# A transformer block on one core: a seventh blocked tile in the MLP's up stage, its weight sums requested before the tile ahead, and the down stage's block sums built later

## The chip, the cores and the metric

The kernel runs on one core of one Trainium2 chip. The metric is the device time of one execution in microseconds (us), as the median of several runs. All arithmetic is in 32-bit floats. The engines of the core are TensorE (PE, the matmuls; PEld is its weight load), VectorE (DVE), ScalarE (ACT), GpSimd (POOL) and SyncE (SP), which here only issues transfers. POOL also issues transfers: those that add to what already lies at the destination.

## The reference

One decoder block over 512 tokens of width 1024: a norm, a mixed attention, a gated MLP with a short causal convolution, and a gate with a second input. The part that matters here is the MLP:

```python
h = rmsnorm(x, mlp_pre_g[i])
gu = h @ w_gate_up[i].astype(h.dtype)          # 1024 -> 2 * 2816
a, u = jnp.split(gu, [D_FF], axis=-1)
a = causal_dwconv(a, conv_w[i], conv_b[i])     # 3 taps along the tokens
y = (jax.nn.gelu(a, approximate=True) * u) @ w_down[i].astype(h.dtype)   # 2816 -> 1024
x = x + rmsnorm(y, mlp_post_g[i])
```

## The kernel before

Data lies transposed: 128 features on the partitions, 512 tokens along the free axis. Each float matrix is kept as two parts, a rounded high part and a remainder, and every product is three matmuls (high by high, low by high, high by low). A weight therefore goes through four steps: a load into a raw place ("wr", two places), the high part by an ACT copy (line 144), the low part by a DVE subtraction (line 148), and then the matmuls (lines 165, 168, 169). The split parts lie in six "wh" places, two for each weight of 1024 columns.

**The up stage** (`mlp_up`) walks over 22 tiles j of 128 features of `w_gate_up`, from about 250 us of the profiled execution on. A *plain* tile has two weights, gate and up, each multiplied in 8 steps of the inner dimension, so 2 x 8 x 3 = 48 matmuls of 512 columns. A *blocked* tile (list `BLOCKED`, line 73) computes the same outputs by the seven-product scheme for a 2 x 2 block of matrices (`blocked_tile`, line 1249): 7 products of 4 steps, 84 matmuls of 256 columns. It needs sums of quarter weights and sums of quarter inputs, and more additions at the end to put the four output blocks together (lines 1268 to 1274). After each tile of either kind come the convolution (ACT line 1155, DVE line 1157 twice), the gelu (ACT line 1158), the product with the other half (line 1177, or 1276 in a blocked tile), and the split of the result y (lines 1163 and 1164).

**The weight sums** of a blocked tile are made by transfers alone (`block_sums_ahead`, line 1205). Two tiles x and y of 512 KB are taken from the places with tag "p" (six). SP loads quarter weights into them (lines 1211 and 1212). Then POOL issues three adding transfers, one after another (`accumulate`, line 1203): y += two quarters from memory, a half of x += a half of y, the other half of x += the first. The three additions are placed behind the last matmul issued so far (`self.pinned`), but that is an order for the planner and no wait on the chip. In `blocked_weights` (line 1235) a blocked tile uses four weights in this order: two raw quarters from memory (line 1239), y, one raw quarter (lines 1241 to 1245), x.

**The down stage** (`mlp_down`) multiplies y by `w_down`. Six of its eight output tiles go in pairs by the same blocked scheme. For one of the pairs the weight sums are prepared in memory (`downblocks`): four copies of 384 KB from memory to memory, issued by SP (`down_copies`, line 1227, through line 291), then four adding transfers from POOL (`down_additions`, line 1233, through line 1203). The third adds what the second has made, and the fourth what the third has made. `group_weights` reads them at line 1076. The kernel before calls two copies after blocked tile 10 and two after blocked tile 12. The additions are called in threes from the end of tile `DOWN_SUMS` on.

**The order.** A planner lays the program out ahead of time. It simulates the engines, takes the ready instruction that stands first in the program, and gives each tile a free place of its tag, or a wait until one is freed. On the chip each engine then works its instructions strictly in that order. An instruction whose input is not there holds up all that stand behind it on its engine. `load_late` (line 291) keeps a transfer behind all that the program has given to SP before it.

**Places.** `SLOTS` gives how many places each tag has. `YTAG` says where the 22 results y lie until the end of the down stage, `PTAG` where the sums of the inputs lie, `TTAG` where the sums of y lie in the down stage. `mlp_down` names tags for the last weights of the down stage and for the first weights of the gate (lines 1381 to 1386).

Of the kernel before, what the change touches and what calls it, by code (L numbers as in the profile page):

```python
# [42 lines left out]
SLOTS = {"u": 26, "kn": 4, "p": 6, "pt": 3, "tt": 2, "wh": 6}  # L43


YTAG = ["u"] * 18 + ["kn"] * 3 + ["p"]


NB = 4
# [16 lines left out]
MP = 3  # L66
ORDER = [[(0,), (), (1, 2)], [(0,), (1, 2), ()], [(0, 1, 2), (), ()]]
STAG = ["u", "u", "u", "tt", "tt", "tt"]
TTAG = ["pt"] * 3 + ["p"] * 5 + ["u"] * 4
LAGS = [(1, 2), (2, 2)]  # L70


BLOCKED = [10, 12, 14, 16, 18, 20]
ROWS = 2048
RAW_LAST = 6
PTAG = ["pt", "pt", "pt", "tt", "tt", "p", "p", "kn"]
AHEAD = 8
DOWN_SUMS = 16
DRAM_SUMS = 1


class Block:
# [977 lines left out]
    def sums_of(self, i):  # L1060
        f = self.u([P, 2, T], F32, STAG[i])
        for k in range(2):
            y = self.y[2 * i + k]
            self.nc.vector.tensor_add(f[:, k, :], y[:, 0, :].bitcast(F32), y[:, 1, :].bitcast(F32))
        self.tt.append([self.u([P, 2, T], F32R, t) for t in TTAG[2 * i : 2 * i + 2]])
        for _ in self.half_sums([[f[:, k, hs] for hs in HALF] for k in range(2)], self.u([P, 4, H], F32, STAG[i]), self.tt[i]):
# [93 lines left out]
    def keep_y(self, j, c):  # L1160
        nc = self.nc
        y = self.u([P, 2, T], F32R, YTAG[j])
        nc.scalar.activation(y[:, 0, :], c, AF.Copy)
# [41 lines left out]
    def block_sums_ahead(self, j):  # L1205

        gs = self.io["gs"][BLOCKED.index(j)]
        two = lambda t: t.rearrange("p (s n) -> p s n", s=2)
# [26 lines left out]
    def blocked_weights(self, j):  # L1235

        nc, gs = self.nc, self.io["gs"][BLOCKED.index(j)]
        x, y = self.ahead_sums.pop(j)
# [58 lines left out]
    def mlp_up(self):  # L1297
        self.phase = "mlpup"
        nc, io = self.nc, self.io
        self.y = []  # L1300
        self.tt = []
        self.hn, self.ht = [], []
        x1 = self.x1
        pss = self.chunkwise(self.upw, self.h2, ("s", "mm", "s", "mm"))
        raws = []
        for i in range(2):
            raws.append(self.u([P, D], F32, "p"))
            self.load_late(raws[i], io["gu"][NB + 2 + i])
        ahead = [self.weight(io["gu"][NB + i], keep=True) for i in range(2)]
        ahead += [self.weight(r, early=True) for r in raws]  # L1310
        self.spill()
        cyc = itertools.cycle(["s", "o", "t", "t", "s", "mm", "s", "mm"])
        pp = {}
        n = 0
        self.ahead_sums = {}
        todo = self.normalized(x1)
        copies, adds = self.down_copies(), None
        for j in range(NB // 2, NFF):
            if j == AHEAD:
                self.block_sums_ahead(BLOCKED[0])  # L1320
            if j in BLOCKED:
                for _ in todo:
                    pass
                self.blocked_tile(j, [next(cyc) for _ in range(4)])
                if j != BLOCKED[-1]:
                    self.block_sums_ahead(BLOCKED[BLOCKED.index(j) + 1])
                for _ in range(2):
                    next(copies, lambda: None)()
            else:
                x = self.h2 if j <= RAW_LAST else self.hn  # L1330
                for i in range(2):
                    wt = ahead.pop(0) if ahead else self.weight(io["gu"][2 * j + i])
                    ps = self.ps(next(cyc))
                    self.ordered = n < 4
                    self.gemm(ps, wt, x)
                    self.ordered = False
                    pp[i] = ps
                    if n == 0:
                        self.r3 = self.row_rstd(self.row_sums(self.acc3), "r3")
                        for k in range(NB // 2):  # L1340
                            self.mlp_tile(k, pss[2 * k], pss[2 * k + 1])
                    n += 1
                    if n > 1:
                        for _ in range(1 if j <= RAW_LAST else 2):
                            next(todo, None)
                self.mlp_tile(j, pp[0], pp[1])
            if j >= DOWN_SUMS:
                for c in copies:
                    c()
                adds = adds or self.down_additions()  # L1350
                self.pinned = self.last
                for _ in range(3):
                    next(adds, lambda: None)()
                self.pinned = None
        for a in adds:
            a()

    def mlp_down(self):
        self.phase = "mlpdown"
        nc, io = self.nc, self.io  # L1360
        acc = self.s([P, T])
        yo = [self.u([P, 2, T]) for _ in range(4)]
        ks = [range(0, 8), range(8, 16), range(16, NFF)]
        self.pgw = []
        self.rawtag = itertools.cycle(["wr", "wr", "kn"])
        for c in range(2 * MP, KC - 1):
            m = yo[c // 2][:, c % 2, :]
            ps = self.ps("mm")
            for n, k in enumerate(ks):
                wt = self.weight(io["down"][c][:, k.start * P : k.stop * P], len(k) * P)  # L1370
                self.gemm(ps, wt, [self.y[j] for j in k], k.start == 0, k.stop == NFF)
                self.sums_of(n)
            nc.vector.tensor_copy(m, ps)
            self.square_acc(acc, m, True)
        for c in range(0, 2 * MP, 2):
            self.pair_of_tiles(c, yo[c // 2], acc)

        c = KC - 1
        keep = self.tc.keep_in_program_order
        wts = []  # L1380
        for k, t in zip(ks, ("wr", "wr", "u")):
            n = len(k) * P
            wts.append(self.weight(self.raw(io["down"][c][:, k.start * P : k.stop * P], n, t), n, early=True))
        for n, tag in enumerate((("p", "tt"), ("pt", "pt"), ("kn", "tt"))):
            self.pgw.append(self.weight(io["wpg"][n], tag=tag))
        raw = self.raw(io["wpg"][3])
        self.e = self.unspill("e", ["pt", "u", "u", "u"])

        def last(h, js, ps):
            for j in js:  # L1390
                self.mm3(ps, wts[j // 8], j % 8 * P, self.y[j][:, :, HALF[h]], j == 0, j == NFF - 1, keep=True)

        def out(h, ps):
            m = yo[c // 2][:, c % 2, HALF[h]]
            sq = self.s([P, H])
            keep(nc.scalar.activation(sq, ps, AF.Square))
            keep(nc.vector.tensor_copy(m, ps))
            a = acc[:, HALF[h]]
            keep(nc.vector.tensor_add(a, a, sq))
            return a  # L1400

        ps0, ps1 = (self.ps(t)[:, HALF[h]] for h, t in enumerate(("s", "mm")))
        last(0, range(NFF), ps0)
        a0 = out(0, ps0)
        last(1, range(5), ps1)
        y = self.rstd_col(a0, "r4a")
        last(1, range(5, 10), ps1)
        r = self.rstd_row(y, "r4a", copy=False)
        self.pgw.append(self.weight(raw, early=True, keep=True))
        last(1, range(10, NFF), ps1)  # L1410
        self.phase = "norm"
        self.x2 = []
        run = lambda gen, n: [next(gen, None) for _ in range(n)]
        first = self.norm_half(0, r, C_GMPOST, yo, self.x1, self.x2)
        run(first, 4)
        a1 = out(1, ps1)
        self.pss = [self.ps(t) for t in ("s", "s", "s", "mm")]
        run(first, 1)
        self.gate_half(0, range(0, 3))
        y = self.rstd_col(a1, "r4b")  # L1420
        run(first, 2)
        self.gate_half(0, range(3, 5))
        r = self.rstd_row(y, "r4b", copy=False, tag="o")
        run(first, 2)
        second = self.norm_half(1, r, C_GMPOST, yo, self.x1, self.x2)
        run(second, KC + 1)
        self.gate_half(0, range(5, KC))
        self.gate_half(1, range(KC))
# [36 lines left out]
    def run(self):  # L1465
        self.consts()
        self.attention()
        self.tc.cur_priority = LATE
        self.out_proj()
        self.mlp_up()  # L1470
        self.mlp_down()
        self.ple_gate()
# [62 lines left out]
```

## Time and profile before

| what | value |
|---|---|
| runs shown | 660.81, 660.32 and 664.28 us, median 660.81 |
| profiled execution | 660.37 us, its span 658.7 us |
| busy DVE, ACT, POOL | 74%, 54%, 26% of the span |
| DMA over the span | 93.37 MB, mean 142 GB/s |
| up stage, tiles 10 to 21 | 360.0 to 490.6 us of the span |
| down stage and the rest | from 490.6 us on |

A profile line of an engine names the line of the code, the engine and the operation, then what is written and read by the program's names with numbers left out, and the shape: `mlpup_wh<-mlpup_wr` is a split weight made from a raw one, `mlpup_u` any tile of the pools "u", "p", "kn", "pt" or "tt", `in_gs_dram` the quarter weights of blocked tiles, `in_gu_dram` those of plain tiles. `[2.79 <-DMA ...]` is idle time in front of an instruction, and what ended it. SPq and POOLq are the issuing queues of SP and POOL. A row of the chain of waits has a start, a length, and what took it. A row of transfers has a count, the size of one and the median us from issue to landing.

### The profile page before, as it was taken

The numbers are of one execution on the slowest core, as the hardware profiler recorded it, in microseconds if no ns is written. First come the engines' busy times: TensorE is split into PE (matmuls) and PEld (weight loads), VectorE is DVE, ScalarE is ACT, GpSimd is POOL, SyncE is SP. The second block draws the span as 40 slices with busy tenths as digits, with TensorE's granted clock in tenths as the row PEclk, the third lists the DMA queues.
The fourth block names the chain that finished last, engine by engine and source line by source line (L and its number), as shares of the span: only waits on it lengthen the run. The fifth ranks groups of instructions, "written<-read, shape, count | busy, mean of one in ns | idle before, by whom it ended". The sixth has DMA issues, their size and how long they took to land.

```text
span 658.7 us, 10426 instructions
## 1 busy us (share of the span) xinstructions
PE 647.8 (98%) x3665; PEld 562.9 (85%) x3665; DVE 485.2 (74%) x995; ACT 357.8 (54%) x664; POOL 171.5 (26%) x253
## 2 busy tenths in 40 slices
PE   9999999999999999999999999989999999999997
PEld 8988878878888888888888988879988899999986
DVE  6795687978756469689998576477699775856873
ACT  7464687978887476345556245345544443334351
POOL 1111597678486060002221112101000010201000
PEclk9999999999999999999999999999999999999999
DMA  8436721212264437321259976985252434387032
GB/s 303 158 115 202 199 66 46 58 27 62 69 210 157 146 102 281 129 96 65 96 144 275 234 178 180 215 228 144 65 144 80 145 89 121 91 279 275 3 112 81
DMA packets 41252, 93.37 MB, mean 142 GB/s; under 512 B 4336, under 2 KB 13680, under 8 KB 40944
## 3 DMA queue, kind: packets, MB, share of 16 engines
q1 hardware_dynamic: 37440, 84.75, 39.7%
q0 software_dynamic: 3616, 7.87, 7.0%
q8 instruction: 29, 0.48, 0.3%
q14 instruction: 23, 0.19, 0.1%
q10 hardware_dynamic: 144, 0.08, 0.1%
HBM read 75.91 MB, written 9.44 MB: 130 GB/s over the span
## 4 chain that ended last, share of the span: by engine, by line
PE 87%; DVE 5%; ACT 3%; DMA 3%; issue 2%; POOL 1%; DVEq 0%; ACTq 0%
PE mlpup_pss L168 3%; PE mlpup_pss L169 3%; PE mlpup_pss L165 3%; DMA mlpup_wr<-in_gs_dram 3%; PE mlpup_pst L165 2%; PE mlpup_pst L168 2%; PE mlpup_pst L169 2%; PE nsa_pso L609 2%; PE nsa_pst L576 2%; PE mlpdown_psmm L165 2%; PE mlpdown_psmm L168 2%; PE mlpdown_psmm L169 2%; PE mlpup_psmm L165 2%; PE mlpup_psmm L168 2%; PE mlpup_psmm L169 2%; PE mlpdown_pst L169 2%
## 5 line engine op out<-in xcount | busy, mean ns | idle before, releaser
L144 ACT ACTIVATE mlpup_wh<-mlpup_wr 128x1024 fp32r<-128x1024 f32 x32 | 33.7, 1055 | 51.4 <-DMA mlpup_wr<-in_gs_dram 30.3
L148 DVE TENSOR_TENSOR mlpup_wh<-mlpup_wr,mlpup_wh 128x1024 fp32r<-128x1024 f32 x32 | 39.9, 1246 | 27.0 <-ACT mlpup_wh L144 23.9
L144 ACT ACTIVATE mlpdown_wh<-mlpdown_wr 128x1024 fp32r<-128x1024 f32 (+1 forms) x27 | 26.7, 989 | 46.9 <-PE mlpdown_psmm L168 11.0
L148 DVE TENSOR_TENSOR mlpdown_wh<-mlpdown_wr,mlpdown_wh 128x1024 fp32r<-128x1024 f32 (+1 forms) x27 | 31.5, 1165 | 20.7 <-ACT mlpdown_wh L144 20.7
L287 POOL TENSOR_TENSOR mlpdown_s<-mlpdown_s,mlpdown_s 128x512 f32<-128x512 f32 x6 | 9.7, 1617 | 137.3 <-ACT mlpdown_s L286 137.1
L599 POOL TENSOR_SCALAR nsa_u<-nsa_u,nsa_nrc,gate 128x512 f32<-128x512 f32 (+3 forms) x64 | 38.6, 615 | 14.7 <-DVE nsa_nrc L735 9.6
L701 ACT ACTIVATE nsa_u<-nsa_u,nsa_nnm 128x512 f32<-128x512 f32 (+3 forms) x64 | 35.4, 555 | 6.8 <-DVE nsa_nnm L694 6.6
L168 PE MATMUL mlpup_pss<-mlpup_u,mlpup_wh 128*128 128x256 f32 (+1 forms) x100 | 33.8, 338 | 2.8 <-DVE mlpup_wh L148 2.8
L581 DVE TENSOR_TENSOR nsa_u<-nsa_pst,nsa_u 128x512 fp32r<-128x512 f32 (+1 forms) x43 | 29.4, 685 | 6.8 <-ACT nsa_u L578 6.5
L165 PE MATMUL mlpup_pss<-mlpup_u,mlpup_wh 128*128 128x256 f32 (+1 forms) x100 | 33.5, 335 | 0.0
L169 PE MATMUL mlpup_pss<-mlpup_u,mlpup_wh 128*128 128x256 f32 (+1 forms) x100 | 33.3, 333 | 0.0
L1158 ACT ACTIVATE mlpup_s<-mlpup_s 128x512 f32<-128x512 f32 x22 | 13.9, 631 | 32.6 <-DVE mlpup_s L1157 32.4
L148 POOL TENSOR_TENSOR fill_wh<-fill_wr,fill_wh 128x1024 fp32r<-128x1024 f32 (+2 forms) x13 | 24.5, 1887 | 26.5 <-ACT fill_wh L144 26.5
L1174 POOL TENSOR_TENSOR mlpup_s<-mlpup_s,r3b 128x512 f32<-128x512 f32 x7 | 11.1, 1580 | 78.0 <-ACT mlpup_s L1158 78.0
L168 PE MATMUL mlpup_pst<-mlpup_u,mlpup_wh 128*128 128x512 f32 (+1 forms) x92 | 31.1, 338 | 0.0
L165 PE MATMUL mlpup_pst<-mlpup_u,mlpup_wh 128*128 128x512 f32 (+1 forms) x92 | 31.1, 338 | 0.0
L169 PE MATMUL mlpup_pst<-mlpup_u,mlpup_wh 128*128 128x512 f32 (+1 forms) x92 | 30.9, 338 | 0.0
L694 DVE CUSTOM_DVE_ANT_0 nsa_u<-nsa_pss,biastables_u 128x224 f32<-128x224 f32 (+3 forms) x64 | 27.8, 447 | 3.0 <-PE nsa_pss L635 2.4
L578 ACT ACTIVATE nsa_u<-nsa_pst 128x512 fp32r<-128x512 f32 x43 | 25.4, 593 | 8.5 <-PE nsa_pst L576 8.1
L168 PE MATMUL mlpup_psmm<-mlpup_u,mlpup_wh 128*128 128x512 f32 (+1 forms) x80 | 26.9, 337 | 0.4 <-DVE mlpup_wh L1245 0.4
L165 PE MATMUL mlpup_psmm<-mlpup_u,mlpup_wh 128*128 128x512 f32 (+1 forms) x80 | 26.9, 337 | 0.2 <-ACT mlpup_wh L1244 0.2
L1203 POOL DMA_DIRECT2D mlpup_u<-mlpup_u x12 | 10.6, 886 | 62.6 <-DMA mlpup_u<-in_gs_dram 30.8
(548 smaller groups left out, 2350.9 us busy)
## 6 DMA issues: line engine op xcount, KB each, us to landing
mlpup_wr<-in_gu_dram SPq DMA_DIRECT2D x26, 512.0 KB, 3.3
mlpup_u<-in_gs_dram SPq DMA_DIRECT2D x12, 512.0 KB, 4.6
mlpdown_wr<-in_down_dram SPq DMA_DIRECT2D x7, 512.0 KB, 3.6
fill_wr<-in_win_dram SPq DMA_DIRECT2D x6, 512.0 KB, 3.7
mlpup_u<-in_gs_dram POOLq DMA_DIRECT2D x6, 512.0 KB, 7.1
mlpup_u<-mlpup_u POOLq DMA_DIRECT2D x12, 256.0 KB, 3.7
mlpup_wr<-in_gs_dram SPq DMA_DIRECT2D x6, 512.0 KB, 6.1
fill_u<-fill_u SPq DMA_DIRECT2D x20, 128.0 KB, 2.7
```

Source lines behind the costliest of these rows:

```text
L144: h = nc.scalar.activation(hi, raw, AF.Copy)
L148: l = eng.tensor_sub(lw, raw, hi.bitcast(F32))
L165: r = self.pin(mm(ps, hi, x[:, 0, :], start=start, stop=False))
L168: mm(ps, lo, x[:, 0, :], start=False, stop=False)
L169: self.last = mm(ps, hi, x[:, 1, :], start=False, stop=stop).ins
L576: self.att(nc.tensor.transpose(pt[:, r * P : (r + 1) * P], src, self.ident))
L578: nc.scalar.activation(t[:, 0, :], pt, AF.Copy)
L581: nc.vector.tensor_sub(t[rs, part, :], pt[rs], t[rs, 0, :].bitcast(F32))
L599: self.nc.gpsimd.tensor_scalar(ap, ap, col, gate, op0=ALU.mult, op1=ALU.mult)
L694: nc.vector.tensor_tensor_reduce(dst, src, dist, op0=ALU.add, op1=ALU.min, scale=SLOPES[8 + 4 * g + r], scalar=start, accum_out=out)
L701: nc.scalar.activation(dst, dst, AF.Exp, bias=nm[:, r, b : b + 1], scale=-1.0, accum_out=sm[:, r, b : b + 1])
L1158: nc.scalar.activation(c, c, AF.Gelu_apprx_tanh)
```

## The change

- `BLOCKED` has seven tiles instead of six: 10, 12, 13, 15, 16, 18, 20. Tile 14 becomes plain, and 13 and 15 become blocked, so 12 and 13 are neighbours, and 15 and 16.
- In `mlp_up` the sums of the next blocked tile are asked for before `blocked_tile` and not after it. When they are asked for, the tile ahead still holds its own x and y.
- The two calls of copies after a blocked tile go. `DOWN_SUMS` goes from 16 to 18, and there all four copies are called at once, at the end of tile 18, with three additions behind them, and the fourth at tile 19.
- Tags: y of tile 17 lies in "kn" instead of "u", and y of tile 20 in "p" instead of "kn". One sum tile of the down stage goes from "p" to "u". The third raw weight of the last down tile goes from "u" to "tt", and the first gate weight from "p" and "tt" to "u" and "u".
- The host lays out `in_gs_dram` for seven tiles (line 1507, which reads the list).

```diff
-YTAG = ["u"] * 18 + ["kn"] * 3 + ["p"]
+YTAG = ["u"] * 17 + ["kn"] * 3 + ["p"] * 2
...
-TTAG = ["pt"] * 3 + ["p"] * 5 + ["u"] * 4
+TTAG = ["pt"] * 3 + ["p"] * 4 + ["u"] * 5
...
-BLOCKED = [10, 12, 14, 16, 18, 20]
+BLOCKED = [10, 12, 13, 15, 16, 18, 20]
...
-DOWN_SUMS = 16
+DOWN_SUMS = 18
...
-                self.blocked_tile(j, [next(cyc) for _ in range(4)])
                 if j != BLOCKED[-1]:
                     self.block_sums_ahead(BLOCKED[BLOCKED.index(j) + 1])
-                for _ in range(2):
-                    next(copies, lambda: None)()
+                self.blocked_tile(j, [next(cyc) for _ in range(4)])
...
-        for k, t in zip(ks, ("wr", "wr", "u")):
+        for k, t in zip(ks, ("wr", "wr", "tt")):
...
-        for n, tag in enumerate((("p", "tt"), ("pt", "pt"), ("kn", "tt"))):
+        for n, tag in enumerate((("u", "u"), ("pt", "pt"), ("kn", "tt"))):
```

## The prediction

> **What bounds the kernel now.** I read the page's busy times first, then a table of busy time cut at the starts of the up stage's tiles, then the chain of waits, then the transfers.
>
> ```profile
> PE 647.8 (98%) x3665; PEld 562.9 (85%) x3665; DVE 485.2 (74%) x995; ACT 357.8 (54%) x664; POOL 171.5 (26%) x253
> ```
>
> TensorE (PE) is busy for 647.8 of 658.7 us. Only two things can shorten the kernel: fewer matmul columns, or less of PE's lost time. The next rows are tiles 12 to 19 of the up stage, one row each. The columns are the stretch, its length, then busy time and instruction count of PE, PEld, DVE, ACT and POOL, the granted clock, the DMA share and GB/s.
>
> ```profile
> 380.92:392.06 11.14, 10.29 (x86) 10.08 (x85) 8.41 (x11) 6.57 (x10) 1.22 (x1) 1.00 0.61 151
> 392.06:402.96 10.90, 10.90 (x50) 9.02 (x49) 6.19 (x11) 3.49 (x5) 1.77 (x2) 1.00 0.84 220
> 402.96:413.47 10.51, 10.28 (x86) 10.07 (x84) 8.21 (x10) 5.94 (x9) 2.92 (x3) 1.00 0.69 150
> 413.47:424.38 10.91, 10.91 (x51) 9.02 (x50) 4.10 (x8) 1.77 (x2) 1.75 (x2) 1.00 0.96 241
> 424.38:437.84 13.46, 11.15 (x85) 10.30 (x84) 9.20 (x12) 7.07 (x11) 2.70 (x3) 1.00 0.90 224
> 437.84:448.75 10.91, 10.91 (x51) 9.02 (x49) 8.56 (x12) 5.13 (x7) 1.17 (x2) 1.00 0.80 197
> 448.75:458.74 9.99, 9.99 (x85) 9.99 (x84) 7.67 (x12) 4.91 (x7) 0.86 (x1) 1.00 0.48 130
> 458.74:469.65 10.91, 10.91 (x51) 9.02 (x49) 7.99 (x11) 5.31 (x8) 0.00 (x0) 1.00 0.26 75
> ```
>
> A plain tile (48 matmuls of 512 columns) takes 10.91 us. A blocked one (84 of 256) takes 9.99 us when nothing waits, as tile 18 does. Tiles 12, 14 and 16 take 11.14, 10.51 and 13.46: they lose 1.15, 0.52 and 3.47 us, together 5.14. The clock is 1.00 throughout, so these are waits. The chain says for what:
>
> ```profile
> 390.32 6.94 DMA mlpup_wr<-in_gs_dram
> ...
> 411.73 9.93 DMA mlpup_wr<-in_gs_dram
> ...
> 433.73 1.23 DVE mlpup_wh L148
> 435.00 0.39 PE mlpup_pss L168
> ```
>
> A 9.93 us load of a blocked tile's raw weights stands ahead of the late split on DVE (L148) for which PE waits at 435.00. ACT is the link. In the list of waits from 340 to 440 us it stands idle for such loads:
>
> ```profile
> ACT mlpup_wh L144 <- DMA mlpup_wr<-in_gs_dram: 24.3, 3, 9.2
> ```
>
> While ACT waits, the convolution and gelu of the tiles before stand queued behind the split, and then everything comes at once. The loads themselves are slow because of what is in flight beside them. The transfers issued from 364 to 369 us, and then from 399 to 414 us, with the median us to landing last:
>
> ```profile
> downblocks<-in_gd_dram SPq DMA_DIRECT2D x2, 384.0 KB, 6.5
> ...
> mlpup_wr<-in_gs_dram SPq DMA_DIRECT2D x1, 512.0 KB, 8.4
> ```
>
> ```profile
> downblocks<-in_gd_dram POOLq DMA_DIRECT2D x2, 384.0 KB, 8.9
> ...
> mlpup_wr<-in_gs_dram SPq DMA_DIRECT2D x1, 512.0 KB, 9.9
> ```
>
> In the first group the down stage's copies run beside the load of tile 12, in the second its additions beside the load of tile 16.
>
> **The change, part by part.**
>
> *One more blocked tile.* The list goes from six to seven. PE gains 10.91 - 9.99 = 0.92 us.
>
> *Weight sums ahead.* The call moves in front of the tile. What it can change shows in the timeline:
>
> ```profile
> 357.57 1.23 DVE L148 TENSOR_TENSOR mlpup_wh<-mlpup_u,mlpup_wh 128x1024 fp32r<-128x1024 f32 x1 [0.26 <-ACT mlpup_wh L144]
> ...
> 358.83 0.38 SPq L1211 DMA_DIRECT2D mlpup_u<-in_gs_dram  x1
> ...
> 379.72 0.87 POOL L1203 DMA_DIRECT2D mlpup_u<-mlpup_u  x1 [2.79 <-DMA mlpup_u<-mlpup_u]
> ...
> 401.77 1.04 ACT L144 ACTIVATE mlpup_wh<-mlpup_u 128x1024 fp32r<-128x1024 f32 x1
> ```
>
> ```profile
> mlpup_u<-mlpup_u POOLq DMA_DIRECT2D x12, 256.0 KB, 3.7
> ```
>
> The load at 358.83 starts 0.03 us after the split of tile 10's sum has ended (357.57 + 1.23), and it is for tile 14. Tile 12's places are already taken. So the trace already runs two blocked tiles ahead, in four of the six "p" places, and the moved call finds the same place free at the same moment. I take nothing for it, gain or loss. Its cover: tile 14's last addition is issued at 379.72 and lands 3.7 us later, at 383.4, 24.6 us after the first load; the sums are first split at 401.77, 18 us after that. In the new list that place goes to tile 13, due one plain tile (10.91) and tile 12's saved wait (1.15) earlier, so 6 us are left. Tiles 15, 16 and 18 likewise come 2 x 9.99 + 10.91 = 30.9 us after the tile whose places they take, against the 24.6 needed. If that cover went, PE would lose each sum's lateness in full. On POOL, additions of two tiles stand in order behind each other; on SP the two loads stand ahead of the tile's own raw loads, as they do now.
>
> *Copies and additions to tile 18.* These rows give first and last starts:
>
> ```profile
> L291 SPq DMA_DIRECT2D downblocks<-in_gd_dram x4: 508/578/1418, 346.9 to 366.8; - x4
> L1076 SPq DMA_DIRECT2D mlpdown_u<-downblocks x3: 367/409/462, 488.9 to 518.6; - x3
> ...
> L1203 POOL DMA_DIRECT2D downblocks<-downblocks x2: 807/984/1161, 421.5 to 427.5; - x2
> ```
>
> Four copies on SP and four additions on POOL leave the stretch 347 to 428 us. The copies now follow tile 18's raw loads on SP. The chain has the raw load of tile 16 at 411.73, 12.7 us before that tile; tile 18 starts at 448.75 - 5.14 - 0.92 = 442.7 in the new time, so the copies go out from about 430 us, at the latest with the tile. Two additions follow, then one, then one: 430 + 6.5 + 3 x 8.9 = 463 us for the last landing, at the latest 476. The first reader, at 488.9 now, comes at 483 at best. I cost them at nothing: 7 to 20 us cover them, and beyond that every us late would be PE's. What they free is most of the 5.14 us, but tiles 18 and 20, which lose nothing now, get the traffic.
>
> *Neighbouring blocked tiles, 12 with 13 and 15 with 16.* This is the new load. A blocked tile moves 512 + 256 KB of raw weights, three times 512 KB for its sums, and twice 256 KB between places: 2.9 MB. A plain one moves 1.05 MB. Tiles 12 to 16 are four and one, 12.6 MB in 4 x 9.99 + 10.91 = 50.9 us: 248 GB/s. In the table, 241 GB/s had a DMA share of 0.96 and the slowest load. So the removal of the down traffic is partly refilled. I bound the new loss s: 0 as in tile 18, or 3.47 in each of 13, 15, 16 and 18 as in tile 16, so 13.9 us. Nearest are tiles 12 and 14, whose loads took 8.4 and 6.94 us without the pile-up of tile 16; their mean loss is (1.15 + 0.52)/2 = 0.84. I take that for 13, 15 and 16, and 0 for 12 (its copies are gone), 18 and 20: s = 2.5.
>
> Where a page disagrees: the Trainium skill, "DMA: Bandwidth & Descriptors", Specifications, gives some 358 GB/s of memory bandwidth for a core. By that, 248 would be two thirds of what is there, no load would queue, and s would be 0. The row with 0.96 at 241 GB/s speaks against it here, so I do not take it as the forecast.
>
> *Places by other tags.* One y from "u" to "p", one sum tile from "p" to "u", one raw weight to "tt", one gate weight to "u": the same work in as many places. The cover is the same idle ACT and DVE in the down stage; I take nothing.
>
> **The sum.** The profiled execution took 660.37 us, its span 658.7; the median of the three runs is 660.81, 0.44 above. Relative to the median: 660.81 - 0.92 - 5.14 + 2.5 = 657.25, so 657.2.
>
> **The rivals.**
>
> 1. *The transfers stay quick, full gain.* s = 0: 660.81 - 6.06 = 654.8. For it: the down traffic goes, and tile 13's raw loads are issued into a quiet stretch (0.61 in the row of tile 12). Against: 248 GB/s. This is the skill's case above.
>
> 2. *DVE takes the place of the load.* The rows by shape for 392 to 413 us:
>
> ```profile
> L148 DVE TENSOR_TENSOR mlpup_wh<-mlpup_wr,mlpup_wh 128x1024 fp32r<-128x1024 f32 x4 | 4.9, 1223 | 5.5 <-ACT mlpup_wh L144 5.5
> ...
> L1274 DVE TENSOR_TENSOR mlpup_s<-mlpup_pso,mlpup_s 128x512 f32<-128x512 f32 x1 | 0.7, 682 | 0.0
> ...
> L1269 DVE TENSOR_TENSOR mlpup_s<-mlpup_s,mlpup_pss 128x256 f32<-128x256 f32 x1 | 0.4, 414 | 0.0
> ```
>
> A blocked tile has one wide split, three instructions of 512 and three of 256 columns more than a plain one: 1.22 + 3 x 0.68 + 3 x 0.41 = 4.5 us. Tiles 12 to 19 in the table have 60.3 us of DVE for four pairs, 15.1 each, so a plain tile has 5.3 and a blocked one 9.8, beside PE's 9.99. If DVE also stands idle for 2.3 us a tile, as in tile 18's row (9.99 - 7.67), the second tile of each pair is 2.1 us late: 4.2 us, with 0.84 each for 15 and 18 s = 5.9, and the time 660.7. Against: the gaps can be filled by splits, and plain tile 14 lets DVE catch up.
>
> 3. *Slower: the raw loads queue behind the sums through the whole stretch.* ACT waits at 13, 15, 16 and 18 as it did at 16, 3.47 us each: 654.75 + 13.9 = 668.6. It decides from s = 6.06 us on. For it: 248 GB/s, and only two raw places, refilled about 10 us ahead. Against: the down traffic that made tile 16 so slow is gone, and a load that waits longer needs over 10 us to hurt.
>
> **How the numbers follow.** Forecast with partial gain 0.55; full gain 0.15; DVE 0.20; slower 0.10. The range 654.8 to 662.0 starts at s = 0 and ends at 3.47 in both 15 and 16 (654.75 + 6.94, 661.7, rounded up); about 2 in 10 lie outside. Within 1%, about what a measurement here can tell from no change, means 654.2 to 667.4. Faster by more needs idle time that no term here holds: 0.04. Slower by more is half of rival 3: 0.05. Same: 0.91.
>
> **What would show it.** The changed table should have seven blocked rows. Right: 12 near 9.99, and 13, 15 and 16 below 11.2; DMA share above 0.85 from 12 to 16; ACT's total wait for raw blocked loads below 24.3 us. Wrong: any blocked row above 13, PE waiting on a downblocks load in the down stage, a POOL addition that ends after its split is due, or the row of 18 as slow as that of 16 was. An up stage under 125 us from tile 10's start on would be the full gain.

## The result, and the profile after

| | median us | runs from to | profiled execution | its span |
|---|---|---|---|---|
| before | 661.11 | 660.32 to 664.28 | 660.37 | 658.7 |
| after | 654.33 | 654.24 to 654.43 | 654.41 | 652.7 |

The ratio is 0.9889, with a 95% interval of 0.9856 to 0.9921. The changed kernel is faster by 1.1%. The forecast of 657.2 was wrong, and 654.33 lies 0.5 us below its range. The first rival, the full gain at 654.8, came closest.

The first row of the page after gives the busy times of the engines:

```profile
PE 645.0 (99%) x3701; PEld 563.1 (86%) x3701; DVE 489.3 (75%) x1002; ACT 359.7 (55%) x667; POOL 174.4 (27%) x256
```

Next are tiles 12 to 19 of the up stage after, one row each, with the columns of the table in the prediction. The sum below them is that of all twelve tiles, 10 to 21.

```profile
380.38:390.84 10.46, 10.26 (x85) 10.05 (x84) 8.97 (x12) 5.80 (x9) 1.22 (x1) 1.00 0.70 143
390.84:400.84 10.00, 10.00 (x86) 10.00 (x85) 8.33 (x12) 5.94 (x8) 2.04 (x3) 1.00 1.00 336
400.84:411.75 10.91, 10.91 (x50) 9.02 (x49) 8.12 (x13) 4.53 (x6) 1.87 (x2) 1.00 0.83 171
411.75:421.74 9.99, 9.99 (x85) 9.99 (x84) 7.55 (x12) 4.90 (x7) 2.09 (x2) 1.00 0.90 205
421.74:431.74 10.00, 10.00 (x86) 10.00 (x85) 6.25 (x9) 5.44 (x8) 1.59 (x3) 1.00 0.93 288
431.74:442.65 10.91, 10.91 (x50) 9.02 (x49) 10.08 (x15) 5.06 (x8) 1.41 (x2) 1.00 0.97 276
442.65:452.64 9.99, 9.99 (x85) 9.99 (x84) 8.27 (x13) 5.06 (x7) 3.47 (x4) 1.00 0.80 164
452.64:463.55 10.91, 10.91 (x50) 9.02 (x49) 5.52 (x7) 4.39 (x6) 1.57 (x2) 1.00 0.89 218
...
sum 124.97, PE 124.77 PEld 115.10 DVE 93.95 ACT 59.22 POOL 19.14; mean PE 10.40 PEld 9.59 DVE 7.83 ACT 4.93 POOL 1.60
```

Only tile 12 still loses anything, 10.46 - 9.99 = 0.47 us. Before, the same twelve tiles took from 360.02 to 490.55, so 130.53 us; now they take 124.97. These 5.56 us are the whole effect of the change: what comes after the up stage takes 168.1 us before (658.7 - 490.6) and 168.2 us after. The other 0.5 us between the two spans stands ahead of tile 10, which begins at 359.48 and not at 360.02. No part of the change lies there, and that start moves by as much from one kernel to the next in all the experiments below.

The heavy traffic that the prediction feared did come: over tiles 12 to 16 the DMA engines move 227 GB/s at a share of 0.87. Tile 13 runs at a DMA share of 1.00 and 336 GB/s, tiles 16 and 17 at 0.93 and 0.97. ACT still stands idle for raw weights of blocked tiles (its waits from 340 to 440 us):

```profile
ACT mlpup_wh L144 <- DMA mlpup_wr<-in_gs_dram: 13.5, 3, 8.2
```

That was 24.3 us in three waits before. Of the 13.5 us, 8.2 are in front of the split of tile 12, 4.3 of tile 15 and 1.0 of tile 18. The raw load of tile 12 still took 8.06 us to land; those of 13, 15, 16 and 18 took 3.41, 5.87, 3.66 and 4.19. So some loads still come late, and PE hardly notices. Why is the question for the experiments.

### The profile page after: what moved, and what is told of

It reads as the page before. It is cut to its first block, busy times and chain, and to the rows that moved or that the text cites. A ratio compares the mean times of both kernels' runs of the same rounds, so it can differ in the third digit from the quotient of the medians.

```text
span 652.7 us, 10523 instructions
## 1 busy us (share of the span) xinstructions
PE 645.0 (99%) x3701; PEld 563.1 (86%) x3701; DVE 489.3 (75%) x1002; ACT 359.7 (55%) x667; POOL 174.4 (27%) x256
## 4 chain that ended last, share of the span: by engine, by line
PE 89%; DVE 4%; ACT 3%; DMA 2%; issue 1%; POOL 1%; ACTq 0%; DVEq 0%
PE mlpup_pss L168 4%; PE mlpup_pss L169 4%; PE mlpup_pss L165 4%; PE mlpup_psmm L165 3%; PE mlpup_psmm L168 3%; PE mlpup_psmm L169 3%; PE nsa_pso L609 2%; PE nsa_pst L576 2%; PE mlpup_pst L168 2%; PE mlpup_pst L165 2%; PE mlpdown_psmm L165 2%; PE mlpup_pst L169 2%; PE mlpdown_psmm L168 2%; PE mlpdown_psmm L169 2%; PE mlpdown_pst L169 2%; PE mlpdown_pst L168 2%
## 5 line engine op out<-in xcount | busy, mean ns | idle before, releaser
L168 PE MATMUL mlpup_pss<-mlpup_u,mlpup_wh 128*128 128x512 f32 (+1 forms) x108 | 36.6, 339 | 0.2 <-DVE mlpup_wh L148 0.2
L165 PE MATMUL mlpup_pss<-mlpup_u,mlpup_wh 128*128 128x512 f32 (+1 forms) x108 | 36.5, 338 | 0.0
L169 PE MATMUL mlpup_pss<-mlpup_u,mlpup_wh 128*128 128x512 f32 (+1 forms) x108 | 36.4, 337 | 0.0
L1203 POOL DMA_DIRECT2D mlpup_u<-mlpup_u x14 | 12.4, 885 | 79.1 <-DMA mlpup_u<-mlpup_u 29.0
L168 PE MATMUL mlpup_psmm<-mlpup_u,mlpup_wh 128*128 128x512 f32 (+1 forms) x88 | 29.9, 340 | 0.0
L169 PE MATMUL mlpup_psmm<-mlpup_u,mlpup_wh 128*128 128x512 f32 (+1 forms) x88 | 29.9, 340 | 0.0
L165 PE MATMUL mlpup_psmm<-mlpup_u,mlpup_wh 128*128 128x512 f32 (+1 forms) x88 | 29.9, 340 | 0.0
L168 PE MATMUL mlpup_pst<-mlpup_u,mlpup_wh 128*128 128x256 f32 (+1 forms) x88 | 26.5, 301 | 0.0
L165 PE MATMUL mlpup_pst<-mlpup_u,mlpup_wh 128*128 128x256 f32 (+1 forms) x88 | 26.5, 301 | 0.0
```

The lines of the kernel that those rows point to most:

```text
L165: r = self.pin(mm(ps, hi, x[:, 0, :], start=start, stop=False))
L168: mm(ps, lo, x[:, 0, :], start=False, stop=False)
L169: self.last = mm(ps, hi, x[:, 1, :], start=False, stop=stop).ins
```

## The experiments

Four theories are tested.

- L, the *late split*: a late raw load hurts only through what stands behind its split on ACT and DVE.
- D, *traffic*: crowded transfers cost PE time wherever they are.
- C: the call for the sums, moved ahead of the tile, is what frees PE.
- O, *order*, formed later: with neighbouring blocked tiles, the moved call acts through the order that the planner lays out, not through the time at which the sums are made.

**A law read from the two traces.** The profile of before shows, in the timeline of ACT around tile 16 (start, length, line, operation; idle time in front in brackets), what a late split holds up:

```profile
421.76 1.06 ACT L144 ACTIVATE mlpup_wh<-mlpup_wr 128x1024 fp32r<-128x1024 f32 x1 [9.25 <-DMA mlpup_wr<-in_gs_dram]
422.73 0.80 ACT L1155 ACTIVATE mlpup_s<-mlpup_s,cols 128x512 f32<-128x512 f32 x1
425.62 0.63 ACT L1158 ACTIVATE mlpup_s<-mlpup_s 128x512 f32<-128x512 f32 x1 [2.09 <-DVE mlpup_s L1157]
...
427.11 0.76 ACT L1155 ACTIVATE mlpup_s<-mlpup_pss,cols 128x512 f32<-128x512 f32 x1
...
430.47 0.63 ACT L1158 ACTIVATE mlpup_s<-mlpup_s 128x512 f32<-128x512 f32 x1 [2.09 <-DVE mlpup_s L1157]
...
431.53 1.04 ACT L144 ACTIVATE mlpup_wh<-mlpup_u 128x1024 fp32r<-128x1024 f32 x1
```

ACT waits 9.25 us for the raw weight of tile 16. Only then come the convolution and gelu of blocked tile 14 (422.73 and 425.62), although DVE had finished the convolution's input at 416.08, those of tile 15, and the last split of tile 16 (431.53). PE went on with that last weight at 435.00, which is 13.24 us after the late split began. In a tile that loses nothing, PE needs it after five of its seven products, 5 x 1.43 = 7.14 us into the tile. So a split may begin as late as 13.24 - 7.14 = 6.1 us ahead of its tile and cost nothing. The Trainium skill, "PSUM — Partial Sum Buffer", section "Engine vs sequencer instructions", says that ScalarE and VectorE queues are strict FIFO. For ScalarE this trace agrees: the convolution, ready at 416.08, starts at 422.73, 0.97 us after the split, with no idle time of its own.

Call the time from the start of that split to the start of its tile the lead. Then the loss should be 6.1 us minus the lead, where that is positive. For tiles that follow a plain one, with the split in front of the convolution:

| kernel, tile | lead us | 6.1 - lead | loss us |
|---|---|---|---|
| before, 12 / 14 / 16 | 4.95 / 5.59 / 2.62 | 1.15 / 0.51 / 3.48 | 1.14 / 0.51 / 3.48 |
| before, 18 / 20 | 7.20 / 10.10 | none | 0 / 0 |
| after, 12 / 15 / 18 | 5.62 / 7.83 / 9.51 | 0.48 / none / none | 0.47 / 0 / 0 |
| call alone moved, 12 / 14 / 16 / 18 | 6.02 / 5.70 / 5.75 / 5.30 | 0.08 / 0.40 / 0.35 / 0.80 | 0.08 / 0.41 / 0.34 / 0.80 |
| additions alone late, 12 / 18 | 4.67 / 2.60 | 1.43 / 3.50 | 1.44 / 3.50 |

The last two kernels were run after the law was read. Every row fits to 0.01 us. So does tile 12 of three kernels below in which it has this order: leads of 5.93, 4.04 and 5.60 us, losses of 0.18, 2.06 and 0.51 (down part late, list of seven, down part back).

**The parts one at a time.** Each of the first three is the kernel before with one part of the change; the fourth is the changed kernel with one part taken back.

```diff
# copies and additions of the down stage at tile 18
-DOWN_SUMS = 16
+DOWN_SUMS = 18
...
-                for _ in range(2):
-                    next(copies, lambda: None)()
```

> The kernel before, with one part of the change: the down stage's copies and additions are called at tile 18. Theory L (late split): a blocked tile behind a plain one loses 6.1 us minus the lead, where the lead is the time from ACT's start on the split of its first raw weight (line 144) to the tile's start, and nothing if the lead is longer; the rest of the chain is always the same. Tile 16's raw load is no longer beside the additions, so its loss falls from 3.47 us to 0.5 or less; tile 12's load still stands beside the sums of a later tile, so it keeps 0.4 to 1.2, and tile 14 its 0.5. Loss in all 1 to 2.2, time 3 to 4 us below before. Theory D (traffic): loss goes with the mean traffic, which falls in all of the stretch, so all of 5.14 goes, and 18 and 20 start to lose. Theory C (the moved call of the weight sums is what frees PE): nothing changes, 5.14 us stay.

```diff
# the call for the sums ahead of the tile
-                self.blocked_tile(j, [next(cyc) for _ in range(4)])
                 if j != BLOCKED[-1]:
                     self.block_sums_ahead(BLOCKED[BLOCKED.index(j) + 1])
+                self.blocked_tile(j, [next(cyc) for _ in range(4)])
```

> The kernel before, with one part of the change: the weight sums of the next blocked tile are called in front of the blocked tile. Theories L and D: losses stay at 1.15, 0.52 and 3.47 us within 0.5 each, the time that of before within 1 us. Theory C: the 5.14 us go, the time is 5 us below before.

```diff
# the list of seven
-BLOCKED = [10, 12, 14, 16, 18, 20]
+BLOCKED = [10, 12, 13, 15, 16, 18, 20]
```

> The kernel before, with one part of the change: seven blocked tiles 10, 12, 13, 15, 16, 18, 20. Theory L: the second tile of a neighbouring pair (13, 16) loses nothing, since no plain tile's convolution and gelu stand between its splits; 12, 15, 18 and 20 lose 6.1 minus their lead. The additions of the down stage now fall beside the loads of 15 or 18. Loss in all 1 to 5 us, so 1 to 5 us below before. Theory D: 248 GB/s with the down traffic on top, so 13, 15, 16 and 18 lose 2 to 3.5 us each, and the time is 3 to 8 us above before. Theory C: the old loss of 5 stays, only 0.9 us are gained.

```diff
# the changed kernel, copies and additions of the down stage back in their old places
-DOWN_SUMS = 18
+DOWN_SUMS = 16
...
+                for _ in range(2):
+                    next(copies, lambda: None)()
```

> The changed kernel, with its down copies and additions put back to tiles 10, 12 and 16. Theory L: as with the list alone, a loss of 1 to 5 us in tiles that follow a plain one, and 0 in 13 and 16; 655 to 659.5 us. Theory D: 13, 15, 16 and 18 lose 2 to 3.5 us each, 661 to 668. Theory C: the full gain stays, 654.3 within 0.6.

| kernel | median us | ratio to before (95%) | PE's lost time, tiles 10 to 21 |
|---|---|---|---|
| before | 661.2 | | 5.1 us |
| down part late | 657.0 | 0.9921 (0.9893 to 0.9949) | 0.2 |
| call ahead | 656.96 | 0.9946 (0.9920 to 0.9971) | 1.6 |
| list of seven | 659.95 | 0.9965 (0.9949 to 0.9981) | 5.7 |
| after, down part back | 655.05 | 0.9902 (0.9866 to 0.9939) | 0.5 |

The ratios are not the quotients of the two medians. The lost time is the sum of PE's gaps in the profiled execution; that of the down part late was the fastest of its five, 2 us below the median, so the others may lose more. Either of two parts alone takes away most of the old loss, and with the call ahead the down part is worth no more than 0.7 us. The list alone gains its 0.92 us and loses 0.6 us more than before, so that its up stage is 0.3 us shorter; its profiled execution is 1.6 us shorter, and most of the rest lies in an earlier start of the up stage (249.5 and 250.6 us).

None of the three theories had all four right. L and D expected the call alone to gain nothing, and it gained 4.2 us; L expected tiles 13 and 16 of the list of seven to lose nothing, and they lost 1.83 us each; D expected that list to be 3 to 8 us slower than before; C expected the down part alone to gain nothing. And the prediction's account, that the down traffic is the cause and the moved call worth nothing, cannot be whole.

The orders of the engines show how the call alone acts. PE, ACT and DVE keep the order of before in it. On POOL the two first additions of the down stage now stand behind those of tile 18's sums, and on SP the copies behind the raw loads of tile 12. In the trace these additions start at 419.9 us, where before they started at 409.2, just ahead of tile 16's raw load at 411.7; that load now lands in 6.8 us and not in 9.9. Here the call acts through the order of POOL and SP, and by it on when transfers start.

**The additions alone.** If that reading is right, moving these additions and nothing else must move the loss.

```diff
# the kernel before; the copies stay
-DOWN_SUMS = 16
+DOWN_SUMS = 18
```

> The kernel before with DOWN_SUMS = 18 alone: the copies stay behind tiles 10 and 12, and only POOL's additions of the down stage fall behind those of tile 18's weight sums. ACT, DVE, PE and SP keep their orders. Theory L with the two additions as the cause of the late load of tile 16: that load lands in under 7 us and tile 16 loses at most 0.4 us; tiles 12 and 14 keep 1.14 and 0.51; tile 18 may lose up to 0.8 as it did where the call alone was moved. Time 661.2 - 3.1 + 0.5 = 658.6. Rival, that the copies on SP are the cause: tile 16 keeps its 3.48 and the time stays at 661.2.

It took 660.27 us, ratio 0.9998 (0.9979 to 1.0016): no difference, and neither of the two expectations. The table by tile of this kernel, tiles 16 to 18, and the transfers issued from 427 to 434 us say why:

```profile
424.32:434.31 9.99, 9.99 (x85) 9.98 (x84) 7.45 (x10) 5.18 (x8) 2.92 (x3) 1.00 0.65 148
434.31:445.22 10.91, 10.91 (x50) 9.02 (x49) 4.08 (x8) 1.76 (x2) 1.75 (x2) 1.00 0.97 239
445.22:458.71 13.49, 11.20 (x85) 10.31 (x84) 9.53 (x13) 7.67 (x11) 1.69 (x2) 1.00 0.72 160
```

```profile
downblocks<-in_gd_dram POOLq DMA_DIRECT2D x2, 384.0 KB, 9.4
...
mlpup_wr<-in_gs_dram SPq DMA_DIRECT2D x1, 512.0 KB, 10.2
```

Tile 16 is down to 9.99 us, and tile 18 now takes the 13.49. The additions fell beside the raw load of tile 18, which landed in 10.2 us. The 3.5 us moved with them by one pair of tiles. The expectation went by the 0.8 us of the kernel with the call moved, where these additions start 11 us ahead of that load (419.9 and 431.0) and not 2 to 3 us.

**The order alone.** The sharpest test of L against D leaves every transfer in its place in the queues. In the kernel before, the split of a blocked tile's first raw weight is placed behind the convolution of two tiles ahead: an order for the planner, with no wait on the chip. It moves one instruction on ACT and one past two on DVE, at five tiles. PE, POOL and SP keep their orders.

```diff
+        for c, i in zip(behind, (h, l)):
+            self.tc.add_manual_dep(i.ins, c.name, mybir.DependencyInfo(
+                mybir.DependencyClass.NoSync, mybir.DependencyReason.DATA), reason="behind conv")
...
-        yield self.weight(gs[0:2].rearrange("s p n -> p s n"))
+        yield self.weight(gs[0:2].rearrange("s p n -> p s n"), behind=() if j - 1 in BLOCKED else self.convs[j - 2])
```

> The kernel before, with one order changed on ACT and DVE and nothing else: the split of a blocked tile's first raw weight stands behind the convolution of the blocked tile two ahead, not in front of it. Transfers, POOL, SP and PE keep their orders. Theory L (late split: the raw load only hurts because the convolutions, gelus and the last split stand behind it on in-order ACT and DVE): the raw loads land as late as before (8.4, 6.9 and 9.9 us for tiles 12, 14 and 16), the chain behind the split is shorter by about 2.9 us (one convolution and the wait for its two DVE steps), the loss is max(0, 3.2 - lead), so 0, 0 and 0.6 us in place of 1.14, 0.51 and 3.48; the time is 661.2 - 4.5 = 656.7. Theory D (the traffic itself slows PE's stream): same traffic, same losses, 661.2.

It took 655.10 us, ratio 0.9914 (0.9884 to 0.9944): nearly all of the change's gain, with six blocked tiles and the old traffic. The raw loads of tiles 12, 14 and 16 land in 9.3, 7.0 and 9.2 us, where they took 8.4, 6.9 and 9.9. Tiles 12, 14, 15 and 16 in the table by tile:

```profile
380.34:390.33 9.99, 9.99 (x85) 9.99 (x84) 7.31 (x10) 4.90 (x7) 1.66 (x2) 1.00 0.81 219
...
401.24:411.23 9.99, 9.99 (x85) 9.99 (x84) 6.76 (x10) 5.02 (x7) 2.92 (x3) 1.00 0.87 208
411.23:422.14 10.91, 10.91 (x50) 9.02 (x49) 6.13 (x8) 4.53 (x6) 3.11 (x4) 1.00 0.99 237
422.14:432.13 9.99, 9.99 (x85) 9.99 (x84) 6.13 (x9) 4.90 (x7) 1.58 (x2) 1.00 0.95 260
```

No tile loses anything, beside shares of 0.99 and 0.95. Tile 12 is the plainest case: its split began 4.21 us ahead of it, later than the 4.95 us that had cost 1.14 us before, and it cost nothing. ACT around tile 16 (the lines are one to five further down in this kernel, so L145 is the split, L1159 the convolution and L1163 the gelu):

```profile
412.50 0.81 ACT L1159 ACTIVATE mlpup_s<-mlpup_s,cols 128x512 f32<-128x512 f32 x1 [4.28 <-DVE mlpup_s L1277]
417.60 1.06 ACT L145 ACTIVATE mlpup_wh<-mlpup_wr 128x1024 fp32r<-128x1024 f32 x1 [4.28 <-DMA mlpup_wr<-in_gs_dram]
418.57 0.62 ACT L1163 ACTIVATE mlpup_s<-mlpup_s 128x512 f32<-128x512 f32 x1
```

The convolution of tile 14 runs at 412.50, while the load is under way, and its gelu follows the split at once. The split begins 4.54 us ahead of tile 16 (422.14) and costs nothing; by the law above, the old order would have made it cost 1.56. D falls. The time came out 1.6 us below L's own number. Tile 16's split began 4.54 us ahead and not 2.62, as the sum had taken over from before, which is worth its 0.6 us, and the up stage began 0.6 us earlier (250.02 and 250.59); the other 0.4 us are not accounted for.

The same order explains the one exception in the first runs. Where the down part alone was late, tile 18's split began 4.20 us ahead of it and lost nothing; in that kernel the planner itself had put the convolution in front of it.

**What the moved call does.** In the list of seven, two of the blocked tiles follow a blocked one. The changed kernel with the call back behind the tile:

```diff
-                if j != BLOCKED[-1]:
-                    self.block_sums_ahead(BLOCKED[BLOCKED.index(j) + 1])
                 self.blocked_tile(j, [next(cyc) for _ in range(4)])
+                if j != BLOCKED[-1]:
+                    self.block_sums_ahead(BLOCKED[BLOCKED.index(j) + 1])
```

> The changed kernel with the call for the next sums put back behind the tile. Theory L: the places come free at the same moments, the loads and additions start as they do in the changed kernel, only the orders of a few instructions differ, and with the down traffic away no raw load is late: 654.3 to 655.5 us. Theory C (the call ahead is what makes neighbouring blocked tiles possible): tiles 13 and 16 wait for their sums, at least 3 us each, and the time is above 660.

It took 658.49 us, ratio 0.9975 (0.9952 to 0.9998), 4.2 us more than the changed kernel; both expectations missed it. Its ACT around the end of tile 12 and the start of tile 13, and POOL earlier:

```profile
385.35 1.05 ACT L144 ACTIVATE mlpup_wh<-mlpup_wr 128x1024 fp32r<-128x1024 f32 x1
391.88 0.82 ACT L1155 ACTIVATE mlpup_s<-mlpup_s,cols 128x512 f32<-128x512 f32 x1 [5.49 <-DVE mlpup_s L1272]
392.60 0.36 ACT L1268 ACTIVATE mlpup_s<-mlpup_pst 128x256 f32<-128x256 f32 x1
392.87 1.05 ACT L144 ACTIVATE mlpup_wh<-mlpup_u 128x1024 fp32r<-128x1024 f32 x1
```

```profile
363.77 1.21 POOL L1203 DMA_DIRECT2D mlpup_u<-in_gs_dram  x1 [0.36 <-DVE mlpup_u L1164]
```

The sum y of tile 13 was finished by the addition issued at 363.77, which landed 9.2 us later, at 372.9. Its split waits until 392.87, because the convolution of tile 12 stands in front of it, and that needs the end of tile 12. ACT is idle for 5.49 us in between. PE waits 1.83 us in tile 13 and as much in tile 16, and so it does with the list of seven alone. After, with the call in front, ACT has the split of y ahead of that convolution:

```profile
386.26 1.05 ACT L144 ACTIVATE mlpup_wh<-mlpup_wr 128x1024 fp32r<-128x1024 f32 x1
387.21 1.04 ACT L144 ACTIVATE mlpup_wh<-mlpup_u 128x1024 fp32r<-128x1024 f32 x1
```

The additions are placed behind the last matmul that the program has issued when they are called for. Called behind tile 12, they stand at its end in the plan, so the planner takes y for late and puts its split after the convolution. On the chip nothing holds them, and they run at the same time in both (363.8 and 364.8 us). The profiled execution of this kernel took 662.66 us, 4 us above its median, and lost 4.7 us more around tile 18, whose raw load took 12.2 us. Two times 1.83 us are near the 4.2 us of the median, but no execution at the median has a trace. To separate the plan from the place of the call, only the pin was moved:

```diff
# the call stays behind the tile
+                ahead_of = self.last
                 self.blocked_tile(j, [next(cyc) for _ in range(4)])
                 if j != BLOCKED[-1]:
-                    self.block_sums_ahead(BLOCKED[BLOCKED.index(j) + 1])
+                    self.block_sums_ahead(BLOCKED[BLOCKED.index(j) + 1], ahead_of)
...
-        self.pinned = self.last
+        self.pinned = behind or self.last
```

> The changed kernel with the call for the next sums behind the tile again, but its additions placed behind the last matmul ahead of the tile, as where the call stands in front. PE and POOL keep the changed kernel's orders. Theory O (order): what the moved call did was to tell the planner that the sums come early, so that the split of y of tiles 13 and 16 stands in front of the convolution on ACT and DVE and not behind it; the 1.83 us that each of these two tiles lost with the call behind go: 654.3 to 655.0. Rival (the place of the call among the program's loads matters): 658.5 as with the call put back.

654.39 us, ratio 0.9903 (0.9881 to 0.9925), and PE lost 0.06 us in all twelve tiles. At tiles 13 and 16 its orders differ from those with the call put back on PE, ACT and DVE alone; from 427 us on they differ on POOL and SP too. Theory O holds: the moved call is worth 4.1 us in this kernel, all of it through the planner's order. C is right that the call frees PE and wrong in the mechanism: the tiles did not wait for their sums, which were there, but for the split of them.

**Further.** The order was tried on the changed kernel, and more blocked tiles with and without it.

> The changed kernel, with the split of the first raw weight of a blocked tile that follows a plain one behind the convolution of two tiles ahead. Theory L: tile 12's 0.46 us go and nothing else: 654.3 - 0.5 = 653.8. Rival (another wait takes its place): 654.3 or more.

> The changed kernel with eight blocked tiles (10, 11, 13, 14, 16, 17, 19, 20: pairs with one plain tile between) and the convolution kept ahead of the raw split where a plain tile stands between. If the losses stay under 0.5 us in all: 654.3 - 0.92 (one more tile) - 0.47 (tile 12's loss) = 653.0. If three pairs in a row are too much for the transfers (the sums need 24.6 us of loads and additions, and a tile whose places they take is 20 to 31 us ahead): each second tile of a pair waits 2 to 4 us for its sums, and the time is 658 to 664.

> The changed kernel with the list of eight blocked tiles alone, without the order set by hand. Theory L: the raw loads of the tiles behind a plain one (13, 16 and 19) land in 4 to 8 us as with the order set, leads 6 to 9 us, so at most 0.2 us are lost: 653.2 to 653.5. If the order set by hand was what made eight work: above 654.3.

> Nine blocked tiles in threes (10 to 12, 14 to 16, 18 to 20), with the order set by hand. If the transfers still keep up: 653.2 - 0.92 = 652.3. If they do not (the three additions of one tile take 16 to 18 us on POOL in the traces, three tiles of 9.99 and a plain one of 10.91 leave 13.6 each): the third tile of each group waits for its sums, 3 to 10 us in each group, 662 or more.

```diff
# with the order, in the changed kernel; and the lists of eight and nine
+BLOCKED = [10, 11, 13, 14, 16, 17, 19, 20]
...
+BLOCKED = [10, 11, 12, 14, 15, 16, 18, 19, 20]
```

| kernel | median us (from to) | ratio to before (95%) | PE's lost time |
|---|---|---|---|
| after, order by hand | 654.61 (653.73 to 654.84) | 0.9899 (0.9883 to 0.9915) | 0 |
| eight, order by hand | 653.23 (652.90 to 653.60) | 0.9887 (0.9852 to 0.9922) | 0.1 |
| eight | 654.93 (653.79 to 656.31) | 0.9907 (0.9890 to 0.9924) | 2.75 |
| nine, order by hand | 673.84 (670.00 to 674.54) | 1.0181 (1.0154 to 1.0208) | 21.7 |

With the order by hand the changed kernel loses nothing in PE, but its median is not lower: its profiled execution reaches the up stage at 250.71 and not at 250.06 us, so the 0.47 us are below what this start lets one see. Eight blocked tiles with the order have the shortest up stage, 233.13 us against 234.39 after, and a median 1.1 us lower; they did not run in the same group as the changed kernel, and the two ratios cannot be told apart.

Eight without the order lost 2.75 us in its profiled execution, where at most 0.2 was expected. PE, POOL and SP have the same orders in both, but here tile 19's raw load met four copies and two additions at once, and its split began only 1.1 us ahead of the tile. A load that is late enough still costs. The transfers issued from 433 to 441 us:

```profile
downblocks<-in_gd_dram SPq DMA_DIRECT2D x4, 384.0 KB, 6.9
downblocks<-in_gd_dram POOLq DMA_DIRECT2D x2, 384.0 KB, 7.9
...
mlpup_wr<-in_gs_dram SPq DMA_DIRECT2D x1, 512.0 KB, 13.6
```

In the kernel with the order these additions started at 445.4, after a sum's addition that took 9.8 us to land, and the raw load took 7.7. Why they fell differently was not tried. Nine is too many: the waits of ACT from 400 to 505 us name the sums.

```profile
ACT mlpup_wh L145 <- DMA mlpup_u<-mlpup_u: 28.2, 4, 12.6
```

PE lost 7.2 us at once in tile 16 and 5.4 in tile 20, the third tiles of their groups; tile 12, the third of the first group, lost nothing. Behind each of the two waits the granted clock was 0.50 (436.6 to 440.6 and 487.0 to 492.2 us), so that each tile took 10 us too long and not 5 to 7.

## Why the prediction was wrong, point by point

- *One more blocked tile, 0.92 us*: right. Blocked rows are 9.99 to 10.00 us, plain ones 10.91.
- *The losses of 12, 14 and 16 go, 5.14 us*: right but for tile 12, which was to lose nothing without its copies and loses 0.47. Its load still took 8.06 us.
- *Neighbouring tiles lose again, s = 2.5 us*: wrong, and the step that failed. All the losses after are 0.5 us, and 13, 15 and 16 lose 0.02 together; of the 2.9 us between forecast and result, 2.0 are this term. The prediction gave 13, 15 and 16 the mean loss of two tiles behind plain ones whose loads took 8.4 and 6.94 us. The loads of 13 and 16 landed in 3.41 and 3.66 us, 5.7 and 5.5 us ahead of their splits, so that even 8.4 us would have been in time. That of 15 landed in 5.87 us and left a lead of 7.83, where 6.1 are enough. It had seen the queue behind the split, but did not work out from the same rows how late a split may be.
- *The moved call, nothing*: wrong. It looked only at when the sums are made, and there it was right (363.8 and 364.8 us for tile 13). In the old order of ACT, tiles 13 and 16 would have lost 1.83 us each. The prediction saw neither this loss nor that the moved call takes it away; that the two omissions cancel is luck.
- *Down part, "most of the 5.14"*: true alone (5.1 us lost become 0.2 in the trace, 4.2 us off the median), but not needed in the changed kernel: with the down part put back, 0.5 us are lost as with it. The list alone loses 5.7; between these two stand the call and the tags. The copies went out at 433.3 us (430 forecast) and the fourth addition landed at 465.5 (463 to 476); nobody waited for them.
- *Places by other tags, nothing*: no run took the tags alone. The rest of the kernel after the up stage takes 168.2 us and took 168.1.
- *Rival 1*: its time nearly came true, 654.8 against 654.33, and part of its reason: the loads of 13, 15 and 16 were quick. That of 13 ran not beside tile 12 but before it, from 377.1 to 380.5 us. The rule of the Trainium skill, "DMA: Bandwidth & Descriptors", Specifications, that some 358 GB/s are there, would have it that no load queues. The trace disagrees: the raw load of tile 12 took 8.06 us where that of tile 13 took 3.41, and the share of tile 13 was 1.00 at 336 GB/s.
- *Rival 2*: DVE was not the bound. It is busy 8.33 and 6.25 us in the second tiles of the pairs, 13 and 16. *Rival 3*: no tile lost 3.47 us.
- *What would show it*: seven blocked rows, 13, 15 and 16 below 11.2 and ACT's 13.5 us in place of 24.3 came as forecast; tile 12's 10.46 for 9.99 did not, nor a DMA share above 0.85 throughout (0.70 to 1.00). The 124.97 us of the up stage from tile 10 on met the sign named for the full gain.
- *The range*: its lower end was s = 0 and nothing else. The 5.56 us of the up stage alone would give 655.2, inside it. The up stage also began 0.5 us earlier, for no reason in the change, and the median lay 0.44 us above the profiled execution before and 0.08 below it after. Only the two together put the time outside, and that is chance.

## What to carry to other kernels

A late transfer costs what stands behind its first reader on an in-order engine, less the slack to the next use; read both from the timeline before pricing it, and if independent work stands behind the reader, put it in front. An order that only a planner sees, such as a pin behind a matmul, still decides in which order the engines take their work, so a request moved in the program can cost or gain microseconds though the transfers it asks for run at nearly the same times. Ask of a change first which instruction orders it changes, engine by engine.

## What the runs showed that was not expected

- Two adding transfers of 384 KB issued 2 to 3 us ahead of a 512 KB load went with a landing time of 9.93 us (tile 16, before) and 10.2 us (tile 18, with the additions moved there); the load of tile 16 without them took 6.4 us.
- PE runs without a gap beside a DMA share of 0.99 to 1.00 (tile 13 after, tile 15 with the order by hand in the kernel before): the traffic itself took nothing from the matmuls there.
- The start of the up stage differs by up to 1.4 us between kernels whose program up to there has the same work (249.5 to 250.9 us). Gains below half a microsecond have to be read from a stage of the trace.
